# Weight splitting put 100 places later, the keys' table first, and a re-ordered start in a four-layer encoder on one core

## The chip, the cores and the metric

The program runs on one core of a Trainium2 chip, in one launch. The metric is device time in microseconds (us). A core has TensorE (PE), which multiplies matrices into eight PSUM banks, VectorE (DVE), ScalarE (ACT), GpSimd (POOL) and SyncE (SP, which here only issues DMAs). Each engine works through a queue of its own in order and waits on semaphores where an operand comes from another engine or a DMA.

## The reference

The input has 512 tokens of width 1024. It is normalised, and four layers follow, of the kinds A, B, C, A. Every layer projects the tokens, mixes them, attends to 256 memory rows, gates, projects back and normalises:

```python
mkv = mem @ w_mem_kv; mk, mv = split(mkv)          # 256 memory rows, 4 heads
h = layer_norm(x, ln_in_g, ln_in_b)
for i in range(4):
    proj = h @ w_in[i]
    if kind == 0:   branch = fourier_mix(h)        # A
    elif kind == 1:                                # B
        q = axial_rope(rms_norm(q, q_norm_g)); k = axial_rope(rms_norm(k, k_norm_g))
        branch = gqa_block_attention(q, k, v)
    else:           branch = three dilated window attentions, combined   # C
    y = concat(branch, memory_attention(qm, mk, mv)) * silu(gate)
    h = layer_norm(alpha * h + y @ w_out[i], ln_g[i], ln_b[i])
```

## The kernel before

All products run at full float32 precision as three products of halves: an operand `a` is split into a rounded high part `ah` and a low part `al = a - ah`, and `mm3` accumulates `ah*bh + ah*bl + al*bh`. Weights come as 176 chunks of 128 x 1024 numbers, in the order of their use. For each, `fetch` loads the raw chunk (SP queue, two buffers `raw`), ScalarE makes the high part `wh`, and VectorE or GpSimd subtracts to get the low part `wl`: GpSimd takes every third chunk (`i % 3 == 1`) and chunks 2 and 3, in four pieces of 256 columns. A raw buffer is free for the next load when both parts are made.

PE's order is written by hand: the code runs tasks against a rough clock of its own (`Clocks`, with `START` and `ARRIVE` as its guesses of when the first work can begin and when each quarter of `x` arrives), and PE executes in exactly that order. The other four queues are ordered by the framework's scheduler. It gives each instruction a priority by its place in the code, lower places first; `high_priority(offset=-100)` puts the instructions in its scope 100 places later.

The start (function `start`): the memory's transpose `memT` is loaded and split into `memTh` and `memTl`; PE multiplies it by the first two chunks (keys, `mkx` and `mkz`), while VectorE normalises the four 128-token quarters of `x` (statistics `ln_st`, `ln_mv`, `ln_rs`, then one pass with `ln_g` and one with `ln_b`). PE then transposes each quarter (`bank<-ident,x`), ScalarE and VectorE make `hTh` and `hTl` of it, and the first product of layer A (`bank<-wh,hTh`, the DFT chunk) follows. Quarter 0 and 1 are needed first, then quarter 2; from there PE goes on with the layer.

Layer B's entry (`layer_b`): two tables are made on VectorE, `tq` and `tk`, eight products each of the rotary table `rope_b` and a gain vector. The gain tile has one buffer, so `tk`'s gain vector is loaded only after `tq` is done. `use_kv` then runs `norm_rope` for four tiles of keys: on VectorE three products of the PSUM bank with `tk` (tiles `f`), on GpSimd the power of -1/2 of the sum of squares (`nr_s<-nr_s,mhalf`), the addition `f<-f,f` and the scaling `f<-f,nr_s`; then ScalarE rounds to `ks`, GpSimd and VectorE make the two halves of `ksx`, and PE transposes `ksx` and `ks` (`bank<-identr,ksx`). The places in PE's queue at which it does so for tile 0 and tile 1 of the keys are 27 and 36 products of the memory queries' projection after the last product of the keys' and values' projection.

Of the kernel before, what the change touches and what calls it, by code (L numbers as in the profile page):

```python
# [12 lines left out]
F32 = mybir.dt.float32  # L13
# [7 lines left out]
S, D, NMEM = 512, 1024, 256  # L21
# [8 lines left out]
WINDOW = 4  # L30
MARGIN, AMPLE = 1.0, 2.5
LATENCY = {"pe": 0.2, "act": 0.13, "dve": 0.12, "pool": 0.08}
START, ARRIVE = 8.0, (8.0, 12.0, 16.0, 20.0)

BUFS = {
# [287 lines left out]
class Trunk:  # L323
# [118 lines left out]
    def fetch(self):  # L442
        i = self.nchunk
        if i >= self.total:
            return
        self.nchunk += 1
        nc = self.nc
        raw = self.t(self.wpool, [128, 1024], F32, "raw", 2)
        pool, bufs = (self.rpool, 5) if i in self.resident else (self.wpool, 4)
        sl = slice(0, 512 if i in self.dft_chunks else 1024)  # L450
        nc.sync.dma_start(raw[:, sl], self.dram["wall"][i, :, sl])
        wh = self.t(pool, [128, 1024], F32R, "wh", bufs)
        wl = self.t(pool, [128, 1024], F32R, "wl", bufs)
        if i in self.qk_chunks and i % 3 == 0:
            nc.gpsimd.tensor_copy(wh, raw)
        else:
            self.copy(wh[:, sl], raw[:, sl])
        if i % 3 == 1 or i in (2, 3):
            for k in range(0, sl.stop, 256):
                self.sub(wl[:, k:k + 256], raw[:, k:k + 256], wh[:, k:k + 256], nc.gpsimd)  # L460
        else:
            self.sub(wl[:, sl], raw[:, sl], wh[:, sl], nc.vector)
        self.ready.append((wh, wl))

    def chunk(self):
# [61 lines left out]
    def start(self):  # L527
        nc = self.nc
        cp = self.cpool
        self.ident = cp.tile([128, 128], F32, name="ident")  # L530
        self.mhalf = cp.tile([128, 8], F32, name="mhalf")
        nc.vector.memset(self.mhalf, -0.5)
        self.hTh = cp.tile([128, 8, 512], F32R, name="hTh")
        self.hTl = cp.tile([128, 8, 512], F32R, name="hTl")
        self.h_dram = [self.dpool.tile([128, D], F32, name=f"h_dram{t}") for t in range(4)]
        self.mem_dram = [self.dpool.tile([128, 1024], F32, name=f"mem_dram{t}") for t in range(3)]

        with self.tc.tile_pool(name="start", bufs=1, reuse_waits="tile") as sp:
            mkx = sp.tile([128, 4, NMEM], F32R, name="mkx")
            mkz = sp.tile([128, 4, NMEM], F32R, name="mkz")  # L540
            mvv = sp.tile([128, 2, 4, 2, 64], F32R, name="mvv")
            nc.gpsimd.memset(mkz.bitcast(F32), 0.0)
            self.mkx, self.mkz = ([m[:, h] for h in range(4)] for m in (mkx, mkz))
            self.mvv = mvv
            self.fetch()
            mt = self.t(sp, [128, 8, NMEM], F32, "memT")
            for k in range(0, 8, 2):
                nc.sync.dma_start(mt[:, k:k + 2], self.dram["memT"][:, k:k + 2])
            xs = [self.t(sp, [128, D], F32, "x", 4) for _ in range(4)]
            load_x = lambda tt: nc.sync.dma_start(xs[tt], self.rows("x", tt))  # L550
            load_x(0)
            gt, bt = self.load_gb(sp, self.dram["ln_in_g"], self.dram["ln_in_b"], nc.sync)
            self.fetch()
            nc.sync.dma_start(self.ident, self.dram["ident"])
            for tt in range(1, 4):
                self.fetch()
                load_x(tt)
            mh = self.t(sp, [128, 8, NMEM], F32R, "memTh")
            ml = self.t(sp, [128, 8, NMEM], F32R, "memTl")
            for k in range(0, 8, 2):  # L560
                self.copy(mh[:, k:k + 2], mt[:, k:k + 2])
                self.sub(ml[:, k:k + 2], mt[:, k:k + 2], mh[:, k:k + 2])
            self.missing = set(range(4))
            nc.settle(START)
            for tt in range(4):
                nc.chain = ARRIVE[tt]
                self.add(self.layer_norm(sp, xs[tt], gt, bt, xs[tt], tt, False, tt == 3), True)
            self.drive(self.mem_keys(mh, ml))

            def values():  # L570
                yield from self.mem_values(mh, ml)
                for dst, m in zip(self.mem_dram, (mkx, mkz, mvv)):
                    flat = m.rearrange("p a b -> p (a b)") if m is not mvv else m.rearrange("p a b c d -> p (a b c d)")
                    nc.sync.dma_start(dst, flat.bitcast(F32))

            if self.plan[0] == "A":
                self.drive(self.prologue_a(values()))
            else:
                self.drive(values())
                self.prologue(self.plan[0])  # L580
            self.drain()
# [371 lines left out]
        return self.gates(y)  # L953


    def gain_table(self, name, g, scale):

        nc = self.nc
        gt = self.t(self.apool, [128, 64], F32, "gain", 1)
        nc.sync.dma_start(gt, g.partition_broadcast(128))  # L960
        if scale != 1.0:
            nc.vector.tensor_scalar(gt, gt, scale, None, ALU.mult)
        t = self.t(self.apool, [128, 4, 2, 64], F32, name, 1)
        gv = gt.rearrange("p (a b i) -> p a b i", a=2, b=2)
        for tt in range(4):
            nc.vector.tensor_tensor(t[:, tt, 0, :], self.rope[:, tt, 0, :], gt, ALU.mult)
            nc.vector.tensor_tensor(t[:, tt, 1, :].rearrange("p (a b i) -> p a b i", a=2, b=2),
                                    self.rope[:, tt, 1, :].rearrange("p (a b i) -> p a b i", a=2, b=2),
                                    gv[:, :, ::-1, :], ALU.mult)
        return t  # L970
# [41 lines left out]
    def layer_b(self, y):  # L1012
        nc = self.nc
        ap = self.apool
        self.rope = self.t(ap, [128, 4, 2, 64], F32, "rope_b", 1)
        nc.sync.dma_start(self.rope, self.dram["rope_b"])
        tq = self.gain_table("tq", self.dram["q_norm_g"][0], 0.125)
        tk = self.gain_table("tk", self.dram["k_norm_g"][0], 1.0)
        kx = self.t(ap, [128, 4, 512], F32R, "kx", 1)
        kz = self.zero_padded(ap, 512, "kz", 4)  # L1020
        vv = self.t(ap, [128, 4, 4, 2, 64], F32R, "vv", 1)
# [492 lines left out]
                    self.out_proj(y, i, gates)  # L1514


_INS = ["x", "memT", "ln_in_g", "ln_in_b", "q_norm_g", "k_norm_g", "ln_g", "ln_b", "wall"]


def host_arrays(inputs, plan=PLAN):  # L1520
    inp = {k: np.asarray(v) for k, v in inputs.items()}
    a = {
        "x": inp["x"].reshape(S, D),
        "memT": inp["mem"].reshape(NMEM, 8, 128).transpose(2, 1, 0),
        "wall": weight_chunks(inp, plan),
    }
    for n in ("ln_in_g", "ln_in_b", "q_norm_g", "k_norm_g", "ln_g", "ln_b"):
        a[n] = inp[n]
    a.update(constants())
    return {k: np.ascontiguousarray(v) for k, v in a.items()}  # L1530
# [19 lines left out]
```

## Time and profile before

| | us |
|---|---|
| median of 3 runs (1373.86 to 1376.72) | 1375.11 |
| the profiled execution's own time | 1377.85 |
| its span in the trace | 1376.1 |
| PE busy in the span (95%) | 1312.9 |
| VectorE busy (69%) | 947.6 |
| ScalarE busy (46%) | 638.7 |
| GpSimd busy (34%) | 469.8 |

An idle time is shown with the engine that ended it. A row of a timeline has its start, its duration, the engine, the operation and, in brackets, the idle time before it and what ended that. Nearly all rows bear one line number, since one helper records every operation; they are told apart by their tiles.

### The profile page before, as it was taken

The numbers are of one execution on the slowest core, as the hardware profiler recorded it, in microseconds if no ns is written. First come the engines' busy times: TensorE is split into PE (matmuls) and PEld (weight loads), VectorE is DVE, ScalarE is ACT, GpSimd is POOL, SyncE is SP. The second block draws the span as 40 slices with busy tenths as digits, with TensorE's granted clock in tenths as the row PEclk, the third lists the DMA queues.
The fourth block names the chain that finished last, engine by engine and source line by source line (L and its number), as shares of the span: only waits on it lengthen the run. The fifth ranks groups of instructions, "written<-read, shape, count | busy, mean of one in ns | idle before, by whom it ended". The sixth has DMA issues, their size and how long they took to land. (4 is left out here: it accounts for less than half of the span.)

```text
span 1376.1 us, 19720 instructions
## 1 busy us (share of the span) xinstructions
PE 1312.9 (95%) x7312; PEld 1129.2 (82%) x7312; DVE 947.6 (69%) x1635; ACT 638.7 (46%) x1337; POOL 469.8 (34%) x524
## 2 busy tenths in 40 slices
PE   4999998999899899999999999999999999999997
PEld 4988886878788788888889888987888887898886
DVE  6575376476877746667877687897787766657445
ACT  3453323646777631545455355534553644235330
POOL 4204425164201033233522543354335435220421
PEclk8999999999999999999999999999999999999999
DMA  8614333210201253332222232233213325452331
GB/s 290 232 36 179 119 126 118 72 64 19 74 16 33 83 175 118 136 92 70 92 70 92 84 115 70 66 96 93 69 55 108 92 78 184 145 183 75 126 107 61
DMA packets 42863, 141.69 MB, mean 103 GB/s; under 512 B 5640, under 2 KB 6032, under 8 KB 42768
## 3 DMA queue, kind: packets, MB, share of 16 engines
q1 hardware_dynamic: 39888, 130.97, 28.9%
q10 hardware_dynamic: 1728, 5.24, 1.1%
q0 software_dynamic: 1152, 4.23, 0.9%
q8 instruction: 58, 0.95, 0.3%
q14 instruction: 37, 0.30, 0.1%
HBM read 121.80 MB, written 12.06 MB: 97 GB/s over the span
## 5 line engine op out<-in xcount | busy, mean ns | idle before, releaser
L272 PE MATMUL bank<-hTh,wh 128*128 128x512 f32 x832 | 333.2, 401 | 0.0
L272 PE MATMUL bank<-hTh,wl 128*128 128x512 f32 x832 | 326.5, 392 | 0.0
L272 PE MATMUL bank<-hTl,wh 128*128 128x512 f32 x832 | 326.5, 392 | 0.0
L272 POOL TENSOR_TENSOR wl<-raw,wh 128x256 fp32r<-128x256 f32 x242 | 200.0, 856 | 333.6 <-ACT wh L272 246.3
L272 ACT CAST wh<-raw 128x1024 fp32r<-128x1024 f32 x154 | 160.8, 1045 | 205.5 <-PE bank L272 99.2
L272 DVE TENSOR_TENSOR wl<-raw,wh 128x1024 fp32r<-128x1024 f32 x117 | 155.1, 1327 | 139.6 <-ACT wh L272 138.5
L272 PEld LDWEIGHTS bank<-hTh,wl 128*128 128x128 f32 x832 | 157.2, 189 | 34.2
L272 PEld LDWEIGHTS bank<-hTh,wh 128*128 128x128 f32 x832 | 157.7, 190 | 28.4
L272 PEld LDWEIGHTS bank<-hTl,wh 128*128 128x128 f32 x832 | 157.8, 190 | 28.2
L272 DVE TENSOR_TENSOR pt<-bank,pt 128x512 fp32r<-128x512 f32 x160 | 107.3, 682 | 43.2 <-ACT pt L272 42.5
L272 POOL TENSOR_TENSOR f<-f,rope_c 128x256 f32<-128x256 f32 x96 | 94.4, 1005 | 120.3 <-DVE f L272 107.2
L272 PE MATMUL bank<-wh,hTh 128*128 128x256 f32 (+1 forms) x416 | 131.8, 317 | 0.2 <-ACT hTh L272 0.2
L272 PE MATMUL bank<-wl,hTh 128*128 128x256 f32 (+1 forms) x416 | 129.2, 311 | 1.8 <-POOL wl L272 1.8
L272 PE MATMUL bank<-wh,hTl 128*128 128x256 f32 (+1 forms) x416 | 129.3, 311 | 0.2 <-DVE hTl L272 0.2
L272 PE MATMUL bank<-wh,yl 128*128 128x512 f32 x320 | 125.5, 392 | 2.4 <-DVE yl L272 2.4
L272 PE MATMUL bank<-wh,yh 128*128 128x512 f32 x320 | 126.4, 395 | 0.7 <-ACT yh L272 0.7
L272 PE MATMUL bank<-wl,yh 128*128 128x512 f32 x320 | 125.2, 391 | 0.0
L272 ACT CAST pt<-bank 128x512 fp32r<-128x512 f32 x160 | 90.2, 591 | 58.5 <-PE bank L272 56.9
L272 PE MATMUL bank<-ident,p 128*128 128x128 f32 x640 | 91.2, 273 | 3.1 <-ACT p L272 1.5
L272 ACT ACTIVATE p<-bank,nm 128x256 f32<-128x256 f32 (+1 forms) x128 | 74.0, 586 | 40.2 <-DVE nm L272 40.0
L272 POOL TENSOR_TENSOR y<-y,f 128x256 f32<-128x256 f32 x58 | 48.4, 855 | 124.5 <-DVE f L272 113.1
L272 ACT ACTIVATE p<-p,st 128x256 f32<-128x256 f32 x128 | 63.9, 501 | 54.0 <-DVE st L272 53.8
(173 smaller groups left out, 2401.8 us busy)
## 6 DMA issues: line engine op xcount, KB each, us to landing
raw<-wall SPq DMA_DIRECT2D x176, 512.0 KB, 3.5
h_old<-h_dram SPq DMA_DIRECT2D x16, 512.0 KB, 7.0
h_dram<-h_old SPq DMA_DIRECT2D x12, 512.0 KB, 2.7
ck<-cz SPq DMA_DIRECT2D x48, 128.0 KB, 2.8
mem<-mem_dram SPq DMA_DIRECT2D x6, 512.0 KB, 9.5
x<-x SPq DMA_DIRECT2D x4, 512.0 KB, 9.7
h_dram<-x SPq DMA_DIRECT2D x4, 512.0 KB, 3.2
ln_g<-ln_g ACTq DMA_DIRECT2D x4, 512.0 KB, 4.2
```

Source lines behind the costliest of these rows:

```text
L272: return f(*a, **k)
```

## The change

Five edits. In `fetch`, every chunk but the first two makes its `wh` and `wl` 100 places later, and chunks 1 to 4 have their `wl` made by VectorE instead of GpSimd. In `start`, the identity and a compact 128 x 16 tile `gb` of the input norm's two vectors are loaded first; 16 transposes on PE spread them over the partitions, and four ScalarE copies store them, in place of two loads of 512 KB; `x` is loaded before the DFT chunk; `memTl` is made by GpSimd; `START` and `ARRIVE` get other values. In `layer_b`, the keys' gain is loaded first, with a buffer of its own, `tk` is made before `tq`, and `tq` 100 places later.

```diff
+LATER = 100
+START, ARRIVE = 6.0, (10.0, 13.0, 16.0, 18.0)
-START, ARRIVE = 8.0, (8.0, 12.0, 16.0, 20.0)
@@ fetch
-        if i in self.qk_chunks and i % 3 == 0:
-            nc.gpsimd.tensor_copy(wh, raw)
-        else:
-            self.copy(wh[:, sl], raw[:, sl])
-        if i % 3 == 1 or i in (2, 3):
+        with self.tc.high_priority(offset=-LATER if i > 1 else 0):
+            if i in self.qk_chunks and i % 3 == 0:
+                nc.gpsimd.tensor_copy(wh, raw)
+            else:
+                self.copy(wh[:, sl], raw[:, sl])
+            if i % 3 == 1 and i > 4:
...
@@ start
+            nc.sync.dma_start(self.ident, self.dram["ident"])
+            gb = self.t(sp, [128, 16], F32, "gb")
+            nc.sync.dma_start(gb, self.dram["ln_in"])
             self.fetch()
...
-            gt, bt = self.load_gb(sp, self.dram["ln_in_g"], self.dram["ln_in_b"], nc.sync)
             self.fetch()
-            nc.sync.dma_start(self.ident, self.dram["ident"])
             for tt in range(1, 4):
-                self.fetch()
                 load_x(tt)
+            gt = self.t(sp, [128, D], F32, "ln_g", 1)
+            bt = self.t(sp, [128, D], F32, "ln_b", 1)
+            for n, dst in enumerate((gt, bt)):
+                for half in range(2):
+                    ps = self.bank()
+                    for k in range(4):
+                        c = 8 * n + 4 * half + k
+                        self.transp(ps[:, 128 * k:128 * k + 128], gb[:, c:c + 1].to_broadcast([128, 128]))
+                    self.copy(dst[:, 512 * half:512 * half + 512], ps)
+            self.fetch()
+            self.fetch()
...
-                self.sub(ml[:, k:k + 2], mt[:, k:k + 2], mh[:, k:k + 2])
+                self.sub(ml[:, k:k + 2], mt[:, k:k + 2], mh[:, k:k + 2], nc.gpsimd)
@@ layer_b (gains loads a 128 x 64 gain tile, two buffers; gain_table now takes it)
+        gk = self.gains(self.dram["k_norm_g"][0])
         nc.sync.dma_start(self.rope, self.dram["rope_b"])
-        tq = self.gain_table("tq", self.dram["q_norm_g"][0], 0.125)
-        tk = self.gain_table("tk", self.dram["k_norm_g"][0], 1.0)
+        gq = self.gains(self.dram["q_norm_g"][0])
+        tk = self.gain_table("tk", gk, 1.0)
+        with self.tc.high_priority(offset=-LATER):
+            tq = self.gain_table("tq", gq, 0.125)
```

PE's queue has the same instructions but for the 16 transposes of `gb` at its head and three transposes of `x` that stand a few places earlier. On VectorE, ScalarE, GpSimd and SP the order differs in two stretches, the start and layer B's entry, and by one chunk's split that comes two instructions later at layer B's output projection. Three places follow.

VectorE at the start, before: from the second chunk of `x`'s statistics (x_99 is quarter 1, x_100 quarter 2, x_101 quarter 3) to quarter 2's last pass.

```order
L272 BN_STATS ln_st_239<-x_100 128x6 x2
L272 BN_STATS ln_st_257<-x_101 128x6 x2
L272 SCALAR_TENSOR_TENSOR x_99<-x_99,ln_rs_215,ln_b_104 128x1024
L272 BN_AGGR ln_mv_242<-ln_st_239 128x2
L272 TENSOR_TENSOR mkx<-bank_197,mkz 64x256 x2
L272 BN_AGGR ln_mv_260<-ln_st_257 128x2
L272 TENSOR_TENSOR hTl<-bank_250,hTh 128x4x128
L272 TENSOR_SCALAR ln_rs_244<-ln_mv_242 128x1
L272 SCALAR_TENSOR_TENSOR x_100<-x_100,ln_mv_242,ln_g_103 128x1024
L272 TENSOR_SCALAR ln_rs_262<-ln_mv_260 128x1
L272 SCALAR_TENSOR_TENSOR x_101<-x_101,ln_mv_260,ln_g_103 128x1024
```

Now (x_102 is quarter 1, x_103 quarter 2, x_104 quarter 3):

```order
L274 SCALAR_TENSOR_TENSOR x_102<-x_102,ln_mv_245,ln_g_115 128x1024
L274 BN_STATS ln_st_264<-x_104 128x6 x2
L274 TENSOR_TENSOR wl_150<-raw_147,wh_149 128x1024
L274 TENSOR_SCALAR ln_rs_258<-ln_mv_256 128x1
L274 SCALAR_TENSOR_TENSOR x_103<-x_103,ln_mv_256,ln_g_115 128x1024
L274 SCALAR_TENSOR_TENSOR x_102<-x_102,ln_rs_247,ln_b_116 128x1024
L274 BN_AGGR ln_mv_267<-ln_st_264 128x2
L274 TENSOR_TENSOR wl_239<-raw_236,wh_238 128x1024
L274 SCALAR_TENSOR_TENSOR x_103<-x_103,ln_rs_258,ln_b_116 128x1024
```

Subtractions `wl` now stand between the passes over `x`, and the three later `hTl` come behind quarter 2's last pass.

VectorE at layer B's entry, before:

```order
L272 TENSOR_SCALAR gain_1927<-gain_1927 128x64
L272 TENSOR_TENSOR tq_1930<-rope_b_1925,gain_1927 128x64 x8
L272 TENSOR_TENSOR tk_1941<-rope_b_1925,gain_1939 128x64 x8
L272 TENSOR_TENSOR f_1974<-bank_1775,tk_1941 128x8x16 x2
L272 TENSOR_TENSOR f_1973<-bank_1775,tk_1941 128x256
L272 TENSOR_TENSOR wl_1836<-raw_1833,wh_1835 128x1024
```

Now:

```order
L274 TENSOR_TENSOR tk_1945<-rope_b_1939,gain_1940 128x64 x8
L274 TENSOR_TENSOR f_1988<-bank_1789,tk_1945 128x8x16 x2
L274 TENSOR_TENSOR f_1987<-bank_1789,tk_1945 128x256
L274 TENSOR_SCALAR gain_1943<-gain_1943 128x64
L274 TENSOR_REDUCE nr_s_2012<-f_2008 128x4
L274 TENSOR_TENSOR f_2010<-bank_1859,tk_1945 128x8x16 x2
L274 TENSOR_TENSOR f_2009<-bank_1859,tk_1945 128x256
L274 TENSOR_TENSOR f_2119<-bank_1898,tk_1945 128x8x16 x2
L274 TENSOR_TENSOR tq_1955<-rope_b_1939,gain_1943 128x64 x4
```

`tq` moved behind the first eight products of the keys with `tk`; the chunk's subtraction moved further down (it now stands behind the `ksx` of tile 0).

GpSimd at layer B's entry, before: the work between the first power and the casts `ksx` of keys' tile 1 (f_1995, nr_s_1998, ks_323_2007 belong to tile 1).

```order
L272 TENSOR_TENSOR wl_1821<-raw_1818,wh_1820 128x256 x4
L272 TENSOR_TENSOR f_1973<-f_1973,f_1974 128x256
L272 TENSOR_TENSOR f_1973<-f_1973,nr_s_1976 128x256
L272 TENSOR_TENSOR f_1995<-f_1995,f_1996 128x256
L272 CAST ksx_1986<-ks_317_1985 128x2x64 x2
L272 TENSOR_TENSOR f_2104<-f_2104,f_2105 128x256
L272 TENSOR_TENSOR nr_s_1998<-nr_s_1998,mhalf 128x4
L272 TENSOR_TENSOR f_2148<-f_2148,f_2149 128x256
L272 TENSOR_TENSOR nr_s_2107<-nr_s_2107,mhalf 128x4
L272 TENSOR_TENSOR wl_2078<-raw_2075,wh_2077 128x256
L272 TENSOR_TENSOR f_1995<-f_1995,nr_s_1998 128x256
L272 TENSOR_TENSOR wl_2078<-raw_2075,wh_2077 128x256 x3
```

Now (f_2009, nr_s_2012 and ks_328_2021 belong to tile 1), from the first subtraction on:

```order
L274 TENSOR_TENSOR wl_1835<-raw_1832,wh_1834 128x256 x4
L274 TENSOR_TENSOR nr_s_2012<-nr_s_2012,mhalf 128x4
L274 CAST ksx_2000<-ks_322_1999 128x2x64 x2
L274 TENSOR_TENSOR f_2118<-f_2118,f_2119 128x256
L274 TENSOR_TENSOR nr_s_2121<-nr_s_2121,mhalf 128x4
L274 TENSOR_TENSOR f_2009<-f_2009,nr_s_2012 128x256
L274 TENSOR_TENSOR f_2162<-f_2162,f_2163 128x256
L274 TENSOR_TENSOR f_2118<-f_2118,nr_s_2121 128x256
L274 TENSOR_TENSOR wl_2092<-raw_2089,wh_2091 128x256 x4
L274 CAST ksx_2022<-ks_328_2021 128x2x64 x2
```

Both of tile 0's `f` operations and tile 1's addition now stand ahead of the first four subtractions; before tile 1's casts there still stand four subtractions of the next chunk.

## Rows read from the trace of the kernel before

**Rows 1.** Waits of PE over the span: total us, times, longest.
```profile
PE bank L272 <- DVE pt L272: 14.9, 20, 2.9
PE bank L272 <- DVE x L272: 7.6, 2, 6.6
PE bank L272 <- ACT memTh L272: 6.9, 1, 6.9
PE bank L272 <- POOL ksx L272: 5.7, 1, 5.7
PE bank L272 <- ACT wh L272: 4.3, 1, 4.3
```
**Rows 2.** Timeline of PE at the start: start us, us, operation, idle before.
```profile
24.05 1.53 PE L272 MATMUL bank<-ident,x 128*128 128x128 f32 x12 [0.99 <-DVE x L272]
32.19 1.12 PE L272 MATMUL bank<-ident,x 128*128 128x128 f32 x4 [6.61 <-DVE x L272]
```
**Rows 3.** Timeline of VectorE at the start.
```profile
5.51 1.23 DVE L272 TENSOR_TENSOR wl<-raw,wh 128x1024 fp32r<-128x1024 f32 x1 [4.63 <-ACT wh L272]
...
11.03 1.29 DVE L272 BATCH_NORM_STATS2 ln_st<-x 128x6 f32<-128x512 f32 x2 [0.90 <-DMA x<-x]
...
20.11 2.46 DVE L272 BATCH_NORM_STATS2 ln_st<-x 128x6 f32<-128x512 f32 x4
...
24.14 0.86 DVE L272 TENSOR_TENSOR mkx<-bank,mkz 64x256 fp32r<-64x256 f32 x2
...
28.97 1.87 DVE L272 TENSOR_TENSOR hTl<-bank,hTh 128x512 fp32r<-128x512 f32 x3
30.85 1.28 DVE L272 SCALAR_TENSOR_TENSOR x<-x,ln_rs,ln_b 128x1024 f32<-128x1024 f32 x1
```
**Rows 4.** DMA issues, from the page: count, KB, median us to landing.
```profile
raw<-wall SPq DMA_DIRECT2D x176, 512.0 KB, 3.5
...
x<-x SPq DMA_DIRECT2D x4, 512.0 KB, 9.7
```
**Rows 5.** Timeline of GpSimd at the start.
```profile
16.94 5.22 POOL L272 TENSOR_TENSOR wl<-raw,wh 128x256 fp32r<-128x256 f32 x6 [3.56 <-ACT wh L272]
...
34.75 2.38 POOL L272 TENSOR_TENSOR x<-x,ln_b 128x1024 f32<-128x1024 f32 x1
```
**Rows 6.** Timeline of VectorE at layer B's entry.
```profile
219.07 0.56 DVE L272 TENSOR_SCALAR gain<-gain 128x64 f32<-128x64 f32 x1
219.66 1.17 DVE L272 TENSOR_TENSOR tq<-rope_b,gain 128x64 f32<-128x64 f32 x8
223.65 3.40 DVE L272 TENSOR_TENSOR tk<-rope_b,gain 128x64 f32<-128x64 f32 x8 [2.82 <-DMA gain<-k_norm_g]
226.98 0.81 DVE L272 TENSOR_TENSOR f<-bank,tk 128x128 f32<-128x128 f32 x3
```
**Rows 7.** Timeline of GpSimd at layer B's entry.
```profile
223.92 2.92 POOL L272 TENSOR_TENSOR wl<-raw,wh 128x256 fp32r<-128x256 f32 x4 [3.16 <-ACT wh L272]
...
230.85 0.53 POOL L272 CAST ksx<-ks 128x128 fp32r<-128x128 f32 x2
231.34 0.74 POOL L272 TENSOR_TENSOR f<-f,f 128x256 f32<-128x256 f32 x1
232.04 1.07 POOL L272 TENSOR_TENSOR nr_s<-nr_s,mhalf 128x4 f32<-128x4 f32 x1
...
239.39 0.60 POOL L272 TENSOR_TENSOR f<-f,nr_s 128x256 f32<-128x256 f32 x1
239.94 1.58 POOL L272 CAST ksx<-ks 128x128 fp32r<-128x128 f32 x2
```
**Rows 8.** High part of a chunk, from the page: busy, mean ns, idle before.
```profile
L272 ACT CAST wh<-raw 128x1024 fp32r<-128x1024 f32 x154 | 160.8, 1045 | 205.5 <-PE bank L272 99.2
```
**Rows 9.** Timeline of PE at the same place.
```profile
241.28 0.80 PE L272 MATMUL bank<-identr,ksx 128*128 128x128 f32 x4 [5.72 <-POOL ksx L272]
```
**Rows 10.** One stretch: length, busy PE, PEld, DVE, ACT, POOL; granted clock; DMA.
```profile
241.00:247.50 6.50, 6.22 (x19) 5.07 (x20) 1.25 (x5) 2.05 (x7) 3.29 (x8) 0.50 0.43 145
```

More of the change, by code (lines that the diff above doesn't have):

```diff
@@ L453, in fetch @@
         wl = self.t(pool, [128, 1024], F32R, "wl", bufs)
-        if i in self.qk_chunks and i % 3 == 0:
-            nc.gpsimd.tensor_copy(wh, raw)
-        else:
-            self.copy(wh[:, sl], raw[:, sl])
-        if i % 3 == 1 or i in (2, 3):
[L459 to L462, printed above, removed]
+        with self.tc.high_priority(offset=-LATER if i > 1 else 0):
[4 more added lines that the diff above has]
+            if i % 3 == 1 and i > 4:
+                for k in range(0, sl.stop, 256):
+                    self.sub(wl[:, k:k + 256], raw[:, k:k + 256], wh[:, k:k + 256], nc.gpsimd)
+            else:
+                self.sub(wl[:, sl], raw[:, sl], wh[:, sl], nc.vector)
         self.ready.append((wh, wl))
@@ L953, in layer_a, with gains, gain_table @@
         return self.gates(y)
-    def gain_table(self, name, g, scale):
+    def gains(self, g):
+        gt = self.t(self.apool, [128, 64], F32, "gain", 2)
+        self.nc.sync.dma_start(gt, g.partition_broadcast(128))
+        return gt
+    def gain_table(self, name, gt, scale):
         nc = self.nc
-        gt = self.t(self.apool, [128, 64], F32, "gain", 1)
-        nc.sync.dma_start(gt, g.partition_broadcast(128))
         if scale != 1.0:
@@ L1514, in run @@
                     self.out_proj(y, i, gates)
-_INS = ["x", "memT", "ln_in_g", "ln_in_b", "q_norm_g", "k_norm_g", "ln_g", "ln_b", "wall"]
+_INS = ["x", "memT", "ln_in", "q_norm_g", "k_norm_g", "ln_g", "ln_b", "wall"]
 def host_arrays(inputs, plan=PLAN):
@@ L1526, in host_arrays @@
     }
-    for n in ("ln_in_g", "ln_in_b", "q_norm_g", "k_norm_g", "ln_g", "ln_b"):
+    a["ln_in"] = np.concatenate([inp[n].reshape(8, 128).T for n in ("ln_in_g", "ln_in_b")], 1)
+    for n in ("q_norm_g", "k_norm_g", "ln_g", "ln_b"):
         a[n] = inp[n]
```

## Prediction

> **What bounds the kernel now.** I read PE's waits first [rows 1]. PE is busy for nearly the whole span, so time is won only where PE waits or runs at the low clock. Its waits that this change can touch are four: the first operands from ScalarE (6.9 us), the second chunk's high part (4.3), the normalised quarters of x (7.6 in two waits, the longest 6.6), and, late at layer B's entry, the keys' tile from GpSimd (5.7, one wait). The largest item, VectorE's `pt` (14.9 in 20 waits of at most 2.9), lies in the attention stages, where no queue changes its order. Second come the timelines of the two places. At the start, what ends last is the third quarter of x: PE starts its transposes at 32.19 after waiting 6.61 [rows 2], and it ends when VectorE's pass that starts at 30.85 is done; VectorE works from the landing of x at 11.03 with hardly a pause [rows 3]. So the two earlier waits of PE are hidden behind VectorE's chain: PE arrives early at the third quarter anyway. At layer B's entry PE waits from 235.6 to 241.28 for the casts of keys' tile 1 on GpSimd [rows 7, 9], and after that wait its granted clock is 0.50 for the stretch that follows, which is the lower of its two levels, 1.2 GHz [rows 10].
>
> **The start.** Three edits are to be priced together: four chunks' subtractions come to VectorE, `memTl` leaves it, and the norm's vectors are spread by PE.
>
> The chain that decides is VectorE's, from the landing of the first quarter to the last pass over the third. In its new order there stand: eight statistics, 2.46 per four, 4.9; six passes at 1.28, 7.7; three whole subtractions at 1.23 and a half one at 0.6, 4.3; two pairs for the memory's keys at 0.86, 1.7; one `hTl`, 1.87 / 3 = 0.6; some seven small instructions, put at 0.15 each, 1.0. Sum 20.2 us [rows 3]. Before, the same stretch lasted from 11.03 to 30.85 + 1.28 = 32.13, 21.1 us: it held three `hTl` more and no subtraction, with some pauses. The landing itself moves: two small loads (identity and `gb`) now stand ahead on SP's queue, and the transfers behind it are of the same size as before, so I take it 0.7 us later, at 11.7. That gives 31.9 for the third quarter, against 32.13.
>
> `memTl` cost VectorE time only before x landed; it is no part of the chain in either order. On GpSimd, four pieces of 128 x 512 are priced from below by half of the 128 x 1024 addition, 1.2 each, and from above by two of the 128 x 256 subtractions, 2 x 0.87 = 1.7 [rows 5]: PE's first product goes in step with them and ends some 1.5 us later. That costs nothing: the second product, which waited 4.3 us for its chunk [rows 1], gets it sooner, with 1 MB of vectors no longer loaded ahead of it, and both end long before 31.9. The 16 transposes of `gb` are priced by those of x, 1.53 for 12 at the full clock and 1.12 for 4 at the low one: 2 to 4.5 us [rows 2], at a time when PE waits for the first operands. Their load is priced between a chunk's 3.5 and the 9.7 of x in a full queue [rows 4]; with the upper end, the copies of the vectors would come after x lands and VectorE would wait for them, which is the upper bound below.
>
> What is late next: after the third quarter PE needs the second half of the first quarter's `hTl`, which VectorE now makes behind a pass (1.28), a subtraction (1.23) and one other `hTl` (0.6 each), at 31.9 + 3.7 = 35.6. PE has two groups of four transposes, 1.12 each at most, and twelve products to do until then, so it hardly waits for it. I take the start at +0.2 us. From below it could be -3 (VectorE's chain a chunk's subtraction or two shorter than I sum, with x landing earlier because 1 MB less is loaded with it), from above +5 (the vectors or raw chunks late, three subtractions of 1.23 unhidden and some of the waits for them).
>
> **Layer B's entry.** Before, `tk` could not start at 219.66, since its gain vector was loaded into the one buffer only after `tq`; VectorE waited 2.82 for it and then ran eight products in 3.40, because GpSimd's first four subtractions ran beside them, where `tq`'s eight took 1.17 [rows 6]. So the first products `f` came at 226.98. Now `tk` begins where the gain's scaling began, at 219.07, with GpSimd's subtractions still four microseconds away, and takes 1.2: to 220.3. Three products `f` of tile 0 take 0.81, to 221.1, and those of tile 1 as much, after a sum of squares, to 222.5.
>
> GpSimd then does tile 0's addition and scaling (0.74 + 0.60) and tile 1's addition (0.74) from 221.1 to 223.3, that is, before the first four subtractions, which start at 223.92 as before, released by ScalarE's high part and not by anything that moved, and end at 226.84. After them there stand in GpSimd's new order, before tile 1's casts: two powers at 1.07, a pair of casts at 0.53, two additions at 0.74, two scalings at 0.60 [rows 7], together 5.4, to 232.2; and the next chunk's four subtractions, 2.9. These wait for that chunk's high part, so for its load. Its raw buffer comes free when VectorE has made the `wl` that stands behind tile 0's `ksx`. I follow VectorE there: after 222.5 two products `f`, four of `tq`, then four of `tq` beside GpSimd's subtractions at 3.40 / 8 each, and half a dozen instructions of 0.2 to 0.4: 227.3; the subtraction 1.2: 228.6. The load lands 3.5 later [rows 4], at 232.1, ScalarE rounds in 1.05 [rows 8], to 233.2, and GpSimd subtracts until 236.2 [rows 7]. The casts end at 236.8, and PE goes on at 237.0 instead of 241.28. The gain is 4.3 us; the wait falls from 5.7 to 1.4.
>
> A wait of 1.4 us is more like the 0.99 at the start [rows 2] than like the 5.72. I take the clock not to fall: PE was busy for 6.2 us in a stretch at half clock [rows 10], which at the full clock takes 3.1, so 3.1 are won back. Between both ends (nothing, if it falls all the same; 3.1) I take 2.9, since a rest of the stretch may have been at the full clock. `tq` itself is needed only by the queries' norms, further down VectorE's queue, so its delay is hidden.
>
> **The rest.** Of the weights' 100 places nothing else is left in the queues than one split two instructions later at layer B's output projection; PE does not wait there. I put it at nothing. It would cost one wait of a microsecond if that chunk were late.
>
> Sum: +0.2 - 4.3 - 2.9 = -7.0 us, from 1377.85 to 1370.9 for a profiled execution like the one shown. That one stood 2.7 above the median of 1375.11, so the forecast median is 1368.1.
>
> **The rivals.**
> 1. The wait at layer B is shortened, but the clock falls all the same, or the wait stays over 3 us: -1 to -4, 1372.5. For it: the casts wait for a load, a rounding and four subtractions in a row, so 2 us more are easily lost. Against it: each of these steps has a row.
> 2. The start is slower by 4 to 6: VectorE's chain has four subtractions, each behind a load and a rounding; if two of them are late by 2 us, the third quarter is. The sum is then -2.5, 1372.6. For it: the raw chunks have only two buffers. Against it: VectorE reaches each subtraction well after I expect its chunk.
> 3. The start is faster by 3: 1365. For it: 1 MB less is loaded first. Against it: VectorE's own work fills the time.
> 4. Slower than before: GpSimd's four subtractions before tile 1's casts. The order now binds the keys to the next chunk's load. If VectorE's subtraction that frees the raw buffer ends later than 232.9 instead of 228.6, the casts end later than before: 232.9 + 3.5 + 1.05 + 2.9 + 0.5 = 240.9. Every microsecond beyond is lost in full, with the low clock kept; 3 us beyond it, with the start at +0.2, is 1378.3. Traces for it: VectorE's SBUF products do slow beside GpSimd, 0.43 against 0.15 us each [rows 6]. If each of the seven such instructions up to there (four `tq`, two `ksx`, one `wl`) waited out a whole GpSimd subtraction of 0.73, the subtraction would end at 228.6 + 7 x 0.73 - 1.1 already counted = 232.6, just short of that point. The Trainium skill (SBUF — State Buffer, "Who interferes with whom") states such a rule: a VectorE instruction with two SBUF inputs and a GpSimd instruction that reads SBUF exclude each other for the whole instruction. The trace agrees only in part: `tk` slowed by 0.28 per instruction, not by 0.73, as most found the port free.
>
> **How the numbers follow.** The forecast has a chance of 0.56, with a range of its own of 1366 to 1371; rival 1 has 0.12, rival 2 0.14, rival 3 0.06, rival 4 0.12. 0.2%, about what a measurement of this kernel can tell from no change, is 2.75 us. Faster by more: 0.56, 0.07 of rival 1, 0.06 of rival 2 and 0.06: 0.75. Within: 0.05 + 0.08 + 0.02 = 0.15. Slower: 0.10 of rival 4. The range from 1364.5 to 1375.5 leaves out the slower end of rival 4 and a start faster by over 4.
>
> **What would show it.** In the changed profile, PE's transposes of the third quarter should start within 2 us of 32.2, after a wait as long or longer than 6.6, and the sum of PE's waits for x should grow rather than shrink. `tk` should be eight products in about 1.2 us at 219 to 221, measured from the same last product of the keys' projection. PE's wait for `ksx` should be about 1.4, and the stretch after it at the full clock. I am wrong if that wait is over 3 us, if the clock falls after it, if PE meets a new wait for `wl` at the start, or if the third quarter comes after 35.

## The result and the profile after

The changed kernel takes 1367.98 us (median of 4 runs, 1367.26 to 1369.29), the kernel before 1375.19 on the same chip (4 runs): ratio 0.994, interval 0.9925 to 0.9955, which is 8 us less, between 6 and 10. Run once more later it gave 0.9944 (0.9930 to 0.9958). The profiled execution took 1367.26, its span is 1365.5, PE is busy 96% of it.

PE's waits after, which answer to [rows 1] (total us, times, longest):

```profile
PE bank L274 <- DVE pt L274: 15.1, 20, 2.9
PE bank L274 <- DVE x L274: 9.5, 1, 9.5
PE bank L274 <- DMA gb<-ln_in: 3.0, 1, 3.0
PE bank L274 <- POOL ksx L274: 2.1, 1, 2.1
PE bank L274 <- ACT memTh L274: 1.7, 1, 1.7
```

The wait for `ksx` has fallen from 5.7 to 2.1. At the start the small waits (6.9 and 4.3) shrank, and one larger wait for `x` took over most of them, 9.5 where there were 7.6. Up to the third quarter PE's waits sum to 15.8 where they summed to 18.8, and its work grew from 13.2 to 15.2, with the 16 transposes of `gb`. The long wait is now for the second quarter; for the third PE waits 0.6.

PE at the start (answers to [rows 2]); `x8` at 28.52 begins with the second quarter, `x8` at 31.07 with the third:

```profile
28.52 1.97 PE L274 MATMUL bank<-ident,x 128*128 128x128 f32 x8 [9.53 <-DVE x L274]
31.07 1.75 PE L274 MATMUL bank<-ident,x 128*128 128x128 f32 x8 [0.58 <-DVE ln_rs L274]
32.57 0.36 PE L274 MATMUL bank<-wh,hTh 128*128 128x256 f32 x1
```

VectorE there (answers to [rows 3]), and GpSimd's `memTl`, a new row beside [rows 5]:

```profile
11.17 1.29 DVE L274 BATCH_NORM_STATS2 ln_st<-x 128x6 f32<-128x512 f32 x2 [3.59 <-DMA x<-x]
...
24.81 1.21 DVE L274 TENSOR_TENSOR wl<-raw,wh 128x1024 fp32r<-128x1024 f32 x1
...
28.50 1.22 DVE L274 TENSOR_TENSOR wl<-raw,wh 128x1024 fp32r<-128x1024 f32 x1
29.64 1.28 DVE L274 SCALAR_TENSOR_TENSOR x<-x,ln_rs,ln_b 128x1024 f32<-128x1024 f32 x1
```

```profile
8.44 4.98 POOL L274 TENSOR_TENSOR memTl<-memT,memTh 128x512 fp32r<-128x512 f32 x4 [6.75 <-ACT memTh L274]
```

VectorE has no pause from 12.8 us to past the third quarter, as forecast; the third quarter is through at 29.64 + 1.28 = 30.92 (32.13 before), and PE takes it up at 31.07.

Layer B's entry: VectorE (answers to [rows 6]), GpSimd ([rows 7]), ScalarE's rounding of the chunk that GpSimd's second four subtractions wait for, and PE ([rows 9, 10]; the window's columns are length, busy PE, PEld, DVE, ACT, POOL, granted clock, DMA share, GB/s):

```profile
216.95 1.17 DVE L274 TENSOR_TENSOR tk<-rope_b,gain 128x64 f32<-128x64 f32 x8
218.05 0.81 DVE L274 TENSOR_TENSOR f<-bank,tk 128x128 f32<-128x128 f32 x3
...
224.58 1.75 DVE L274 TENSOR_TENSOR wl<-raw,wh 128x1024 fp32r<-128x1024 f32 x1
```

```profile
221.83 3.43 POOL L274 TENSOR_TENSOR wl<-raw,wh 128x256 fp32r<-128x256 f32 x4 [0.27 <-ACT wh L274]
225.21 2.00 POOL L274 TENSOR_TENSOR nr_s<-nr_s,mhalf 128x4 f32<-128x4 f32 x1
...
229.91 1.76 POOL L274 TENSOR_TENSOR f<-f,f 128x256 f32<-128x256 f32 x1
231.64 0.61 POOL L274 TENSOR_TENSOR f<-f,nr_s 128x256 f32<-128x256 f32 x1
232.22 2.94 POOL L274 TENSOR_TENSOR wl<-raw,wh 128x256 fp32r<-128x256 f32 x4
235.10 0.59 POOL L274 CAST ksx<-ks 128x128 fp32r<-128x128 f32 x2
```

```profile
230.68 1.05 ACT L274 CAST wh<-raw 128x1024 fp32r<-128x1024 f32 x1 [0.85 <-DMA raw<-wall]
```

```profile
235.50 0.60 PE L274 MATMUL bank<-identr,ksx 128*128 128x128 f32 x4 [2.08 <-POOL ksx L274]
...
235.50:240.00 4.50, 4.50 (x23) 3.82 (x24) 2.34 (x5) 3.17 (x9) 3.46 (x7) 1.00 0.64 213
```

`tk` is eight products in 1.17, ahead of GpSimd's subtractions. GpSimd then works without a gap up to `ksx`: its row, not the chunk (rounded at 231.73), now ends last. The clock stays at 1.00.

From one profile to the other 10.6 us went: 2.1 up to layer A's exit (first store of `h_dram` at 190.14, then 188.01), 6.4 at layer B's entry (tile 0's transposes to the first scores, 18.77, then 12.36), 1.7 for a fall of the clock at 310 to 320 us that only the execution of before had, 0.4 elsewhere.

### The profile page after: what moved, and what is told of

Read it like the earlier page. It is cut to its first block, busy times and chain, and to the rows that moved or that the text cites. A ratio compares the mean times of both kernels' runs of the same rounds, so it can differ in the third digit from the quotient of the medians.

```text
span 1365.5 us, 19737 instructions
## 1 busy us (share of the span) xinstructions
PE 1309.8 (96%) x7328; PEld 1127.3 (83%) x7328; DVE 945.3 (69%) x1635; ACT 640.6 (47%) x1341; POOL 466.3 (34%) x514
## 4 chain that ended last, share of the span: by engine, by line
PE 72%; DVE 16%; ACT 4%; issue 3%; POOL 3%; DMA 2%; SPq 0%; DVEq 0%; ACTq 0%; POOLq 0%
PE bank L274 72%; DVE f L274 4%; DVE wl L274 2%; DMA raw<-wall 2%; DVE y L274 2%; DVE pt L274 2%; POOL wl L274 1%; ACT p L274 1%; ACT wh L274 1%; DVE nm L274 1%; POOL f L274 1%; DVE cq L274 1%; DVE ck L274 1%; DVE o L274 1%; ACT f L274 0%
## 5 line engine op out<-in xcount | busy, mean ns | idle before, releaser
L274 POOL TENSOR_TENSOR wl<-raw,wh 128x256 fp32r<-128x256 f32 x228 | 186.1, 846 | 319.9 <-ACT wh L274 260.5
L274 DVE TENSOR_TENSOR wl<-raw,wh 128x1024 fp32r<-128x1024 f32 (+1 forms) x121 | 157.7, 1304 | 137.1 <-ACT wh L274 135.9
```

Source lines behind the costliest of these rows:

```text
L274: return f(*a, **k)
```

## The experiments

Each run's profile was read at the same places. Times are us in the span; "tile 0" is PE's start on the transposes of tile 0's `ksx`, "ksx" its start on those of tile 1, "scores" its first product of `qs`; "clock" is the granted clock in the 4.5 us from "ksx" on (6.5 in the first three rows, which is also the stretch of [rows 10]; by stretches of 5 us in the last three).

| kernel | first 128x512 product | wait for `h_old`, layer A's exit | tile 0 | wait for ksx | tile 0 to ksx | clock | ksx to scores |
|---|---|---|---|---|---|---|---|
| before | 52.90 | 0.83 | 232.80 | 5.72 | 8.48 | 0.50 | 10.29 |
| new start only | 51.91 | none | 231.14 | 6.04 | 8.81 | 0.74 (0.63 in 4.5) | 8.89 |
| before, PE kept busy | 52.65 | 1.74 | 233.56 | filled | 9.07 | 1.00 | 7.46 |
| keys first only | 52.79 | 0.98 | 232.78 | 1.78 | 4.54 | 0.62 | 9.17 |
| both gains loaded | 51.30 | 1.01 | 231.19 | 2.28 | 5.04 | 1.00 | 7.60 |
| changed | 51.32 | none | 230.66 | 2.08 | 4.84 | 1.00 | 7.52 |
| changed, again | 51.47 | none | 231.22 | 1.78 | 4.54 | 1.00 | 7.59 |
| without 100 places | 51.33 | none | 230.42 | 2.12 | 4.88 | 0.62 | 8.89 |
| `memTl` on VectorE | 52.06 | none | 231.17 | 1.83 | 4.59 | 1.00 | 7.56 |
| norm vectors loaded | 50.53 | 1.22 | 230.84 | 1.80 | 4.56 | 0.63 | 9.14 |
| clock kept thrice | 52.32 | none | 232.15 | 0.24 | 4.75 | 1.00 | 7.58 |
| low parts moved | 52.10 | none | 231.07 | 0.29 | 3.05 | 1.00 | 7.56 |
| chunk 34 on VectorE | 52.48 | none | 232.24 | 0.37 | 3.14 | 1.00 | 7.53 |

**Keys first only.** Before, with layer B's edit alone:

```diff
+        gk = self.gains(self.dram["k_norm_g"][0])
         nc.sync.dma_start(self.rope, self.dram["rope_b"])
-        tq = ...; tk = ...
+        gq = self.gains(self.dram["q_norm_g"][0])
+        tk = self.gain_table("tk", gk, 1.0)
+        with self.tc.high_priority(offset=-100):
+            tq = self.gain_table("tq", gq, 0.125)
```

> The kernel before with the layer B edit alone (keys' gain first, two gain buffers, tk before tq, tq 100 places later). Theory: this edit carries most of the gain. PE's wait for ksx falls from 5.7 to 2.1 us, the clock does not fall after it (2.8 more), so -6.4 us at the softmax of layer B's memory attention and about 1368.8 median. Rival (the start and the 100 places carry it, layer B's wait only moves to another place): the ksx wait shrinks but another wait of 3 to 6 us appears before 300 us, and the median stays within 2 us of 1375.2.

Median 1370.59 against 1376.28 of before, ratio 0.9952 (0.9933 to 0.9971): 6.6 us, the larger part of the change. The wait fell as in the changed kernel, but here the clock fell after it (columns as in the window above):

```profile
237.32 0.67 PE L272 MATMUL bank<-identr,ksx 128*128 128x128 f32 x4 [1.78 <-POOL ksx L272]
...
237.30:241.80 4.50, 4.48 (x16) 3.67 (x17) 2.62 (x5) 2.57 (x7) 3.76 (x7) 0.62 0.66 212
```

**New start only.** The changed kernel with layer B's tables as before (`tq` first, one gain buffer).

> The changed kernel with layer B's tables as before (one gain buffer, tq first). Theory: only the start's gain is left: layer B's entry 2.1 us earlier than before, ksx wait 5.7 again with the low clock behind it; median 1373. Rival (the start carries more): 1370 or less. Prediction as it was written (start +0.2): 1375.4.

1374.81, ratio 0.9987 (0.9977 to 0.9997): 1.8 us, from 0.4 to 3.2. This holds the 100 places too. Its wait for `ksx` is the long one again, 6.04. With keys first only, the two add up to 8.4 of the changed kernel's 8.

**Without 100 places.**

```diff
-        with self.tc.high_priority(offset=-LATER if i > 1 else 0):
+        with self.tc.high_priority(offset=0):
```

> The changed kernel with the weights' high and low parts back at their own places (offset 0). The queues differ from the changed kernel's by one split at layer B's output projection. Theory: the 100 places are worth nothing: 1368.0, within 1.5 us of the changed kernel, each landmark of the trace within 0.5 us up to layer B's output projection. Rival (the title's edit is what frees the evacuations): 3 us or more slower than the changed kernel.

1369.56, ratio 0.9947 (0.9931 to 0.9963), as the changed kernel: the 100 places are worth nothing that shows. Its order in layer B is the changed kernel's, its wait was 2.12, and yet its clock fell.

**Before, PE kept busy.** 60 transposes of the identity ahead of tile 1's, into the bank that these overwrite:

```diff
+            for h in range(60 if tt == 1 else 0):
+                self.tc.nc.tensor.transpose(tr[:, 128 * (h % 4):128 * (h % 4) + 128], self.ident, self.ident)
```

> The kernel before with 60 extra transposes of the identity on PE, ahead of those of keys' tile 1, into the bank that these then overwrite; the wait for ksx itself is kept. Theory: the wait costs twice, once as idle time and once by the clock that falls in it; with PE kept busy for most of the wait, ksx's transposes still start at 241.3, but the 15 products behind them run at 0.227 instead of 0.427 us each: 2.8 us earlier at the softmax, median 1372.4. Rival (the low clock after the wait has another cause than the idle PE, or the 60 transposes last longer than the wait): no gain, 1375 or more.

1374.28, ratio 0.9989 (0.9979 to 1.0): 1.5 us less, from 0 to 2.9, between what the theory and the rival had. PE in place of the wait, and the 6.5 us behind it (columns as above):

```profile
236.16 6.71 PE L1047 MATMUL bank<-ident 128*128 128x128 f32 x60
242.63 0.54 PE L272 MATMUL bank<-identr,ksx 128*128 128x128 f32 x4
...
242.60:249.10 6.50, 6.50 (x35) 5.49 (x34) 2.50 (x4) 3.44 (x9) 2.49 (x6) 1.00 0.34 101
```

With the clock at 1.00 the stretch from `ksx` to the scores takes 7.46 where it took 10.29 [rows 10]. That is the clock's price in the execution of before, 2.8. The transposes lost 0.3 to 0.6 of what they won, since they ended later than the wait had (tile 0 to ksx 9.07 against 8.48 and 8.81).

**Both gains loaded.** Before, with two gain buffers, both loaded at the head; the queries' eight products still ahead of the keys' in the code (one of the keys' slipped ahead of them, at 217.57).

> Before, with two buffers for the 64-value gains, both loaded at the head of layer B; the order of the tables stays (the queries' eight products first, then the keys'). It asks which half of the layer B edit matters: the load that need not wait for the one buffer, or the order of the sixteen products. Theory 'the load': in before the keys' products started 4 us after the queries' because their gain came late; with the load early they follow at once, some 1.3 us later than with keys first, and nearly all of keys-first's gain is there: wait for ksx at tile 1 of 1.8 to 3 us (5.72 before, 1.78 with keys first), ratio to before 0.995 to 0.997. Rival 'the order': the keys' products still come behind eight others and miss the gap before GpSimd's low parts; wait 4 us or more, ratio 0.998 to 1.0.

1370.09, ratio 0.9960 (0.9946 to 0.9974). VectorE and PE:

```profile
218.10 1.17 DVE L272 TENSOR_TENSOR tq<-rope_b,gain 128x64 f32<-128x64 f32 x8
219.19 1.03 DVE L272 TENSOR_TENSOR tk<-rope_b,gain 128x64 f32<-128x64 f32 x7
...
236.23 0.67 PE L272 MATMUL bank<-identr,ksx 128*128 128x128 f32 x4 [2.28 <-POOL ksx L272]
```

The late load in the one buffer was the fault; the order of the sixteen products adds at most half a microsecond (wait 2.28 against 1.78 to 2.12).

**Clock kept thrice.** The changed kernel with 70 such transposes in the start's 9.5 us, 16 ahead of tile 1's `ksx`, 18 ahead of layer B's output projection:

```diff
+    def warm(self, bank, n):
+        for k in range(n):
+            self.tc.nc.tensor.transpose(bank[:, 128 * (k % 4):128 * (k % 4) + 128], self.ident, self.ident)
```

> The changed kernel with transposes of the identity on TensorE, into banks that the next step overwrites, in three of its idle stretches: 70 in the 9.5 us wait at the start, 16 in the 2.1 us wait for ksx in layer B, 18 ahead of layer B's output projection (2.45 us wait for yl there). No other engine's work moves. Theory 'the lost clock is a price of its own': the granted clock then stays at 1.00 through 28 to 33 us, 235 to 245 and 472 to 480; worth some 0.5 to 1 us at the start (the third quarter of x is ready at 31 us and holds the rest), 0 to 1.4 in layer B, 1.5 to 2 at the output projection: 2 to 4 us less than the changed kernel, ratio to before 0.9915 to 0.993. Rival 'the waits set the time, not the clock': VectorE and GpSimd end when they did, the clock gives back under 1 us in all, ratio 0.9935 to 0.995.

1369.22, ratio 0.9950 (0.9938 to 0.9963): nothing gained, as the rival had it. Length, busy PE, granted clock, DMA share, GB/s:

```profile
25.00:30.00 5.00, 2.25 (x19) 0.93 0.79 283
30.00:35.00 5.00, 4.45 (x21) 0.50 0.88 289
...
470.00:475.00 5.00, 5.00 (x34) 0.70 0.87 276
```

At the start PE still waited 1.89 and 1.40 around the quarters of `x`, and the clock fell later (in the changed kernel it was 0.72 from 20 to 25 and 0.50 from 25 to 30) instead of not at all. At the output projection it fell before the transposes, after waits of 0.84 and 0.90 for `pt`, and they ran partly at the low clock. In layer B it stayed up, as it also does in the changed kernel without them.

**Low parts moved, and chunk 34 alone.** GpSimd's second four subtractions in layer B on VectorE; the first of the two kernels also has chunks 3 and 4 of the start on GpSimd:

```diff
-            if i % 3 == 1 and i > 4:
+            if (i % 3 == 1 or i == 3) and i not in (1, 34):     # low parts moved
+            if i % 3 == 1 and i > 4 and i != 34:                # chunk 34 alone
```

> The changed kernel with the low parts of three weight chunks on other engines: chunks 3 and 4 (the two 1.2 us subtractions in VectorE's unbroken row of work from 22 to 31 us) on GpSimd, which idles there, and chunk 34 (GpSimd's four subtractions, 2.94 us, just ahead of the casts that TensorE waits for in layer B) on VectorE. Theory 'the bound stands where the trace puts it': third quarter of x ready 1.5 to 2.4 us earlier (at 28.7 to 29.6 us, with some of it lost to slower VectorE passes beside GpSimd), and layer B's wait for ksx 0.5 to 1.2 us instead of 2.1: 2 to 3.5 us less than the changed kernel, ratio to before 0.992 to 0.993. Rival 'nothing late is gained': the layer norm's -1/2 powers on GpSimd come behind the moved subtractions, and VectorE's casts take the place of GpSimd's; within 1 us of the changed kernel, ratio 0.9935 to 0.995.

> The changed kernel with the low parts of chunk 34 on VectorE, in place of GpSimd's four subtractions (2.94 us) ahead of the casts that TensorE waits for at tile 1 in layer B; the start as in the changed kernel. Theory 'those four are the wait': the wait for ksx falls from 2.08 to 0.3 to 0.5 us as in the run with both moves, the clock stays at 1.00 there, and the time is 1.2 to 2.0 us under the changed kernel's: ratio to before 0.9925 to 0.9935. Rival 'below what shows': the 1.6 us are there in the trace, and executions differ among themselves by more (their clock falls at other places); ratio 0.9935 to 0.995.

1368.57, ratio 0.9945 (0.9933 to 0.9956), and 1368.29, ratio 0.9941 (0.9927 to 0.9955). GpSimd and PE in the second:

```profile
231.51 1.60 POOL L274 TENSOR_TENSOR f<-f,nr_s 128x256 f32<-128x256 f32 x1
233.97 1.41 POOL L274 CAST ksx<-ks 128x128 fp32r<-128x128 f32 x2 [0.86 <-ACT ks L274]
...
235.38 0.63 PE L274 MATMUL bank<-identr,ksx 128*128 128x128 f32 x4 [0.37 <-POOL ksx L274]
```

The four subtractions were the rest of the wait: 1.4 to 1.8 us go in layer B (tile 0 to ksx 3.05 and 3.14 instead of 4.54 and 4.84 in the changed kernel's two executions). In the time that is not to be seen, as the rival of the second had it: the changed kernel beside it took 1366.94. The profile of the second shows where a gain of this size goes. Its tile 0 came 1.0 later than in the changed kernel beside it, so its scores came only 0.4 earlier (242.91 against 243.35), and then its clock fell where that of the other execution did not (PE alone: length, busy PE, granted clock, DMA share, GB/s; chunk 34 on VectorE, then the changed kernel):

```profile
365.00:370.00 5.00, 4.53 (x21) 0.67 0.16 61
...
365.00:370.00 5.00, 4.49 (x30) 1.00 0.17 67
```

By layer B's output projection it was 1.2 behind (470.98 against 469.73). With the two chunks on GpSimd as well, the third quarter was ready at 28.93, 2.0 earlier, as the theory had it, but the start did not gain (52.10). PE then waited for the fourth quarter, whose power stood on GpSimd behind four subtractions that lasted from 28.16 to 33.55:

```profile
37.75 0.66 PE L274 MATMUL bank<-ident,x 128*128 128x128 f32 x4 [1.65 <-POOL x L274]
```

**`memTl` on VectorE.** The changed kernel with that one argument undone.

> The changed kernel with the four subtractions for the memory's low parts back on VectorE; everything else as in it. Theory 'VectorE's row of work sets the start': the four (some 0.65 us each) come ahead of the statistics of the first quarter, the third quarter of x is ready 1.5 to 2.6 us later (32.5 to 33.7 us), time 1.3 to 2.6 us over the changed kernel, ratio to before 0.9955 to 0.9965. Rival 'x's arrival sets it': VectorE stood idle until x landed at 11.2 us, the four fit there, and the time is the changed kernel's within 0.6 us, ratio 0.9938 to 0.9946; GpSimd's 1.25 us each no longer hold the first memory product, which starts up to 0.7 us earlier to no effect on the end.

1368.92, ratio 0.9952 (0.9939 to 0.9965); third quarter at 31.59, where the five executions with the unaltered start had 30.56 to 31.24: 0.4 to 1.0 later. The first 128x512 product, at 52.06, lies within theirs (51.3 to 52.5), so the edit is worth nothing that shows.

**Norm vectors loaded.** The changed kernel with the two 512 KB loads in place of `gb`, its transposes and copies.

> The changed kernel with the input norm's gain and bias again loaded as two 512 KB transfers behind the first quarter of x, in place of the 8 KB load, the sixteen transposes and the four copies; everything else as in it. It asks whether the spreading on chip is what the start's gain (1.8 us by the run of the start alone) rests on. Theory 'the spreading carries it': the other quarters of x land some 2 us later behind 1 MB more, the third quarter is ready at 32.5 us or later (30.6 to 31.1 with the spreading) and the first 512-wide product at 52.5 us or later (51.3 to 51.9); ratio to before 0.9955 to 0.9965. Rival 'VectorE's row of work sets the start': VectorE is busy without a break from 12.8 us on, later quarters only fill in behind, third quarter within 1 us of before, ratio 0.9938 to 0.995. Both expect no wait for h_old at layer A's exit if that goes with the rest of the new start, and 0.8 to 1.7 us of it if it goes with the two big loads.

1369.17, ratio 0.9949 (0.9936 to 0.9962). PE at the third quarter, and at layer A's exit:

```profile
28.18 1.97 PE L274 MATMUL bank<-ident,x 128*128 128x128 f32 x8 [1.11 <-DVE x L274]
...
188.21 0.65 PE L274 MATMUL bank<-ident,h_old 128*128 128x128 f32 x4 [1.22 <-DVE h_old L274]
```

Both expectations missed the third quarter: it came 3 us earlier than with the spreading, since the framework set two whole subtractions fewer ahead of it on VectorE. The time is in the rival's range, so what the spreading on chip is worth does not show. PE's lead of 0.8 to 0.9 (50.53) is then lost at layer A's exit. All five executions with the big loads wait there for `h_old` (0.8 to 1.7 us), none of the eight without:

```profile
188.04 0.66 PE L274 MATMUL bank<-ident,h_old 128*128 128x128 f32 x4
```

That row is the changed kernel's. The queues have the same order in that stretch. The last weight chunk, whose subtraction on VectorE stands ahead of `h_old`, is rounded as soon as it lands: 130.2 to 131.2 us after PE's first 128x512 product in the five, 129.3 to 130.1 in the eight (180.94 in the changed kernel, 183.06 in before). So the landing of the weights goes with the wait. Whether the two loads, 150 us earlier, are its cause, and how, was not found.

**Changed again.**

> The changed kernel once more, for a second profile and for times on the same chip as the other two. Theory 'the clock after a 2 us wait falls in some executions only': the wait for ksx is 2.1 us again, and the clock in 235 to 245 us is either 1.00, as in the first profile, or falls to about 0.7 for some 4 us, and TensorE then reaches the first scores 12.4 or 13.7 us behind tile 0. Rival 'it keeps the clock always, by something in this kernel': 1.00 and 12.4 us. Both expect a ratio of 0.9925 to 0.9955.

1366.94, ratio 0.9944 (0.9930 to 0.9958). The wait was 1.78, and the clock again stayed, as the rival had it; the theory left both outcomes open, so this run does not decide between them:

```profile
235.76 0.67 PE L274 MATMUL bank<-identr,ksx 128*128 128x128 f32 x4 [1.78 <-POOL ksx L274]
...
235.70:240.20 4.50, 4.44 (x23) 3.71 (x24) 2.65 (x5) 3.56 (x8) 3.81 (x8) 1.00 0.66 205
```

## Why the prediction was right, and where it was not

The forecast of -7.0 us was met (the medians differ by 7.2, the ratio gives 8 with 6 to 10). The mechanism of its largest term, the wait for `ksx`, was right. That the sum came out so close is in part luck: two other terms erred against each other, by about 1.6 each.

*The wait for ksx: -4.3, measured -4.0.* Tile 0 to ksx took 8.48 and 8.81 with the old tables, 4.54 to 4.88 (mean 4.66 of six) with keys first. `tk` in 1.2 and the first four subtractions behind it came as worked out. What failed is the row of GpSimd: two powers at 1.07 and additions at 0.74 were put from undisturbed rows; beside VectorE's subtractions one power took 2.00, one addition 1.76 and the first four subtractions 3.43 instead of 2.92. Its work between the two fours took 7.0, not 5.4. So GpSimd was ready for the second four at 232.2, 1.6 after tile 0 instead of 0.6 before it, and the wait was 2.1, not 1.4. VectorE's subtraction that frees the chunk's buffer ended at 226.33, 4.3 ahead of tile 0, as forecast (228.6 against 232.80). From there to the start of the rounding it took 4.35, not 3.5, so the chunk too was late, rounded 1.1 after tile 0 instead of 0.4; but GpSimd was later still.

Rival 4's point, 0.1 behind tile 0, was far off. It put seven instructions of VectorE at a loss of 0.73 each, 5.1. Measured, the four of `tq` lost nothing (0.62 for four), the two of `ksx` 0.7 (1.29 against 0.59 where GpSimd did not subtract) and `wl` 0.5: 1.2, about what the forecast had counted for `tq` alone. The prediction's 0.28 per product of `tk` is a mean over unlike ones. Before, four of the eight took 0.21 to 0.23, and the four that met GpSimd's subtractions 0.76 to 0.78, so those did wait out about a whole subtraction (duration in ns: least, median, most):

```profile
L272 DVE TENSOR_TENSOR tk<-rope_b,gain x8: 211/495/776, 223.7 to 226.8; 128x64 f32<-128x64 f32 x8
```

*The clock: -2.9, measured -2.8 in this pair and -1.3 on average.* The price was right: the execution of before lost 2.8 (10.29 against 7.46). But the old tables do not always lose it all (1.4 with the new start only, whose clock over 4.5 us was 0.63, as after the short waits that lost it), and a wait of about 2 us does not always spare it. Of the seven executions with a wait of 1.78 to 2.28, three lost 1.4 to 1.7 (keys first only, without 100 places, norm vectors loaded), four nothing; those three and three of the four have the same instructions in the same order there, so it is not the order that decides. From ksx to the scores the two executions with the old tables took 9.59 on average, the six with keys first 8.31; with so few executions 1.3 is a rough figure. Rival 1 thus came true in neither execution of the changed kernel, but in three with the same order, at half the price: the forecast took for certain what holds in some executions. What decides it is open.

*The start: +0.2, measured -1.4 in the traces, -1.8 (-0.4 to -3.2) in the times.* This step failed. VectorE's chain ended at 30.92 instead of 31.9, with x landing at 11.17, not 11.7. That is only part of it: over the kernels, PE's first 128x512 product comes at 52.4 with the old start (51.3 to 52.9) and 51.7 with the unaltered new one (51.3 to 52.5), 0.7 less, within the spread. As much again goes up to layer A's exit, from that product to the first transposes of `h_old`: 137.5 with the old start, 136.8 with the new. There the wait for `h_old` is gone, 1.1 on average, of which 0.4 is lost ahead of it. The sum looked at nothing between 36 us and layer B. That the waits for `x` would grow was right, 7.6 to 10.1 (9.5 and 0.6), but the long one stands ahead of the second quarter, and the third is waited for 0.6, not 6.6 or longer.

*The 100 places: 0, measured 0.* The sum of the terms as measured is -4.0 - 1.3 - 1.4 = -6.7.

## What to carry to other kernels

A table whose gain waits for a buffer holds up everything behind it: a second buffer of 32 KB was worth most of this change. A term read from one execution (a clock that fell, a quarter that came late) should be weighed by how often it comes, and a gain at one place followed to the next wait on the same engine, which may swallow it or hand it on. Once single microseconds remain, the traces can show a wait removed that the times cannot.

## What was not expected of the hardware

- Whether the clock falls after a short wait is not fixed by the order of the instructions: after 1.78 us at layer B's entry it fell in one execution (keys first only, 0.62 in the next 4.5 us) and stayed at 1.00 in another (the changed kernel); after 5.72 and 6.04 it fell in both. Nor is it fixed by the program, elsewhere at least. The changed kernel's two executions differ between 10 and 15 us, behind waits of 1.72 and 0.76 in the first and of 1.67 and 0.97 in the second (PE alone: length, busy PE, granted clock, DMA share, GB/s):

```profile
10.00:15.00 5.00, 5.00 (x24) 1.00 1.02 410
...
10.00:15.00 5.00, 4.50 (x25) 0.67 1.02 413
```

- It fell in every profile in two more stretches, layer B's output projection (down to 0.66 by stretches of 5 us between 465 and 490, around waits of 0.8 and 0.9 for `pt` and, but for the kernel with transposes ahead of it, 2.0 to 2.5 for `yl`) and in layer C between 930 and 955 (down to 0.50, around 2.9 for `pt`). In before it also fell to 0.74 at 310 to 315, after waits of 0.97 and 0.86 for `wl`. The changed kernel has such waits (0.77 and 0.86), and no fall there; two of the other kernels fell there too (0.66 and 0.77 at 305 to 310).
- GpSimd and VectorE hold each other up where both work in SBUF, and both can lose. GpSimd's power of -1/2 of 128 x 4 numbers took 1.0 by itself (all rows here are the changed kernel's). At 225.21 it took 2.0: VectorE's subtraction of 128 x 1024 had begun at 224.58 and had 1.1 to go. This subtraction, 1.2 by itself, took 1.75, for the last of GpSimd's four had 0.7 to go when it began. At 229.91 an addition took 1.76 instead of 0.74 behind a subtraction that had 1.2 to go and lost nothing itself. So what was lost here (1.0, 0.5, 1.0) is nearly what the other's instruction still had to run, and it falls on the one that began second. Not every meeting costs: at 236.06 a subtraction ran beside the second half of a power, and neither was longer than by itself. The Trainium skill (SBUF — State Buffer, "Who interferes with whom") calls the pair of ports that the two share an exclusive lock, and has a VectorE instruction with two SBUF inputs contend with a GpSimd instruction that reads SBUF. The three losses agree with that; the pair at 236 shows none.

```profile
229.86 1.23 DVE L274 TENSOR_TENSOR wl<-raw,wh 128x1024 fp32r<-128x1024 f32 x1 [1.52 <-ACT wh L274]
...
236.06 1.23 DVE L274 TENSOR_TENSOR wl<-raw,wh 128x1024 fp32r<-128x1024 f32 x1
```

```profile
235.65 1.01 POOL L274 TENSOR_TENSOR nr_s<-nr_s,mhalf 128x4 f32<-128x4 f32 x1
```
